# One-hot spread of the gates: a fixed order with score tiles between, strided PSUM columns, 52 instead of 43 score tiles ahead

## Chip, cores and metric

One core of one Trainium2 chip. The metric is the device time of one execution in microseconds: 2368.05 us, the median of three runs (2366.97 to 2370.98).

## What is computed

Two transformer blocks over 512 tokens of 1024 features, all in float32 accuracy (a matrix product is three products of high and low halves). The part that matters here is the first block's expert layer, which picks 16 of 16384 experts for each of 8 heads of each token:

```python
def peer_ffn(x, w_q, sub_keys, u, v):
    ...
        q = (xi @ w_q).reshape(n, PEER_HEADS, 2, PEER_KEY_DIM)
        s = jnp.einsum('nhpc,hpkc->nhpk', q, sub_keys).astype(jnp.float32)
        ts, ti = lax.top_k(s, PEER_TOPK)
        ...
        best_s, best_p = lax.top_k(cand_s, PEER_TOPK)
        idx = jnp.take_along_axis(cand_i, best_p, axis=-1)
        gate = jax.nn.softmax(best_s, axis=-1)
        act = jax.nn.gelu(jnp.einsum('nd,nhkd->nhk', xi, u[idx]).astype(jnp.float32), approximate=False)
        return jnp.einsum('nhk,nhkd->nd', (gate * act).astype(xi.dtype), v[idx])
```

An expert's number is 128 i1 + i2, two key numbers.

## The kernel before

The expert layer treats its tokens in two ways. For the first 384 tokens it computes **every** expert: 128 *U passes* (one score tile `pu`, 128 experts by 384 tokens, from the transposed `peer_u`; `upass`, 24 matmuls of 384 columns, then a Gelu on ScalarE) and 128 *V passes* (`vpass`, 18 matmuls of 512 columns into six PSUM accumulators `po`). Between them the scores are multiplied by G, a dense table of gates [i2, i1, token] that is zero nearly everywhere. The last 128 tokens are computed from gathered rows: 256 indirect DMAs (`gath`, tile `gr`, three buffers, issued by GpSimd), each followed by one VectorE operation.

In order of time: *routing* (query projections, scores, top-16; 24 U passes run beside it), the *spread* that builds G, the *V phase*. NG U passes run ahead of the V phase; their scores go to DRAM (`sd`) and come back (`gl`). In the V phase iterations below NG are V passes alone; from then on each iteration is a U pass and a V pass (*mixed*). VectorE's order is written out by hand there: for each iteration the low half `ulo` of a U weight tile, then some gathers' operations, then `ge`, `vlo`, `cl`, which feed the next V pass. The number of gathers per iteration is spread evenly by

```python
        total = (128 - NG) * 2 + NG * WV - GE
            cost += 2 if i >= NG else WV
            while done < min(256, 256 * cost // total):
```

with WV = 0.5 and GE = 4. Every weight tile is loaded raw by SyncE's queue, cast to its high half by ScalarE (`uhi`, `vhi`) and subtracted to its low half by VectorE or GpSimd (`eng`).

The spread (`spread`, L1093 to L1145) builds G from 768 small matmuls: for each token two products (high and low half of the gates) of a one-hot matrix of i2 (`oa`) with a scaled one-hot matrix of i1 (`ob`), 128 by 128 each, in float16. VectorE writes `bh`, `eql`, `bl` for 64 tokens at a time and `oa`, `ob` for 8 (two buffers). Four tokens share one PSUM bank `pq`, each in 128 neighbouring columns; ScalarE copies the bank into `gs` or `gk` with the token innermost, so that neighbouring PSUM columns land 64 elements apart. `gs` and every second block go to DRAM (`gd`). The scheduler of the framework sets the order here; `ahead(1)` offers it 12 U passes between, and `ahead(NG)` the rest.

Of the kernel before, what the change touches and what calls it, by code (L numbers as in the profile page):

```python
# [20 lines left out]
D = 1024  # L21
# [10 lines left out]
# the even tokens, and the odd ones  # L32
# [133 lines left out]
def _nabias(rpb):  # L166
    """[4 blocks, 8 heads, 128 queries (c, r), 256 keys (c, r)]: the bias, or NEG outside the window"""
# [14 lines left out]
def _sib():  # L182
    """pairs (j, i) whose blocks of s are siblings, s = 1..32"""
    j = np.arange(128)[:, None]
    i = np.arange(128)[None, :]
    return np.stack([(((j // s) ^ (i // s)) == 1).astype(np.float32) for s in (1, 2, 4, 8, 16, 32)], 1)


def program(tc, a, dbg=None):
# [54 lines left out]
    def rstd_of(pool, ps, n, feat, eps, tag="rs", bufs=1, b=None):  # L244
        """-2 feat / sqrt(ps / feat + eps), with one Newton step; the gains carry the factor -1 / (2 feat)"""
# [10 lines left out]
    def warm_rs(after):  # L256
        """the table of the norms, ahead of one"""
# [6 lines left out]
    # ---------------------------------------------------------------- first block, mixing  # L264
# [11 lines left out]
    NG = 43  # L276
    GT = 3
    GN = 3
    OAN = 8
    PQB = 6  # L280
    # the order of the first projection's parts; the last one runs after the others' pools are closed
# [20 lines left out]
    with ExitStack() as es:  # L302
# [10 lines left out]
        def ada_steps():  # L313
            """the conditioning columns: products of rows of the transposed weights with the vectors, and their sums"""
# [29 lines left out]
        def weights():  # L344
            """the next tile of weights; the ones after it are on their way"""
# [14 lines left out]
        # the norm's factor scales the products' columns; the operands hold the gains alone  # L360
# [26 lines left out]
        def rs_columns():  # L387
            """the factor of a token's row, for tiles that have the tokens on the partitions"""
# [14 lines left out]
        def rotate(raw, j):  # L403
            """rotary embedding of a projected tile"""
# [103 lines left out]
        for o in order[:NT]:  # L508
            if o == 'z':
                x0.close()  # L510
                zp = x0.enter_context(tc.tile_pool(name="z", bufs=1, reuse_waits="tile"))
                # lambda
# [8 lines left out]
                V.tensor_scalar(lam, lam, 0.8 - 0.6, -1.0, op0=OP.add, op1=OP.mult)   # -lambda  # L521
# [14 lines left out]
        # ------------------------------------------------ gated linear attention, both directions  # L536
# [12 lines left out]
        def gla_pair(hp):  # L549
# [9 lines left out]
            def diag(h):  # L559
                """the 128 x 128 blocks on the diagonal of A^T"""  # L560
# [79 lines left out]
            # the meta tokens: forward, from the end of their decay to the start of the sequence  # L640
# [42 lines left out]
    # ------------------------------------------------ conditioning of the second block  # L683
# [6 lines left out]
    scl = const.tile([128, 3, KT], F32, name="scl")   # norm gain * (1 + scale): latent 1, context, latent 2  # L690
# [48 lines left out]
        # ------------------------------------------------ differential attention  # L739
# [123 lines left out]
    def shifted(pool, src, n, sc_, sh, rs, hi, lo):  # L863
        """src * gain * rs + shift in two halves"""
# [21 lines left out]
    with ExitStack() as es:  # L886
# [5 lines left out]
        # the context: its norm now, its keys and values behind the output projection  # L892
# [54 lines left out]
    # ------------------------------------------------ experts: scores and routes  # L947
# [20 lines left out]
    # ------------------------------------------------ experts: every expert for the first 384 tokens  # L968
# [10 lines left out]
    def upass(i):  # L979
        wh, wl = us.pop(i)  # L980
        p = psU.tile([128, ND], F32, name="pu")
        for k in range(KT):
            w_ = (wh[:, k * 128:k * 128 + 128], wl[:, k * 128:k * 128 + 128])
            mm3(p, w_, (hn[0][:, k, :ND], hn[1][:, k, :ND]), k == 0, k == KT - 1)
        ge = up.tile([128, ND], F32, name="ge", bufs=4)
# [6 lines left out]
    with ExitStack() as es:  # L992
# [7 lines left out]
        def route(h):  # L1000
            """the 16 best pairs of a head, as two key numbers, for every token"""
            tf = wp.tile([128, 4, 2, 16], BF16, name="tf")
            V.tensor_copy(tf, ti[:, :, 2 * h:2 * h + 2])
            # a pair (a, b) of ranks can be among the best 16 only if (a + 1) (b + 1) <= 16
# [28 lines left out]
            for c in range(2):  # L1033
                # the best 8 have ranks below 8
# [35 lines left out]
        # gates: a softmax over the 16 of each head, the first of which is the largest  # L1070
# [6 lines left out]
    # the last 64 tokens' part stays on chip  # L1077
# [13 lines left out]
    def spread(nt):  # L1091
        """G[i2, i1, n], through DRAM: a sum of products of one-hot rows, the gates scaled and in two halves"""
# [4 lines left out]
        # i1 = 16 a + b; every number twice, so that the last step of an operand is one element  # L1097
        iu = rp.tile([128, 2, 128], U32, name="iu", bufs=1)
        V.tensor_copy(iu[:, 0], p[:, 0:128])
        V.tensor_scalar(iu[:, 1], iu[:, 0], 15, None, op0=OP.bitwise_and)  # L1100
        tw = [rp.tile([128, 128, 2], F16, name=f"tw{j}", bufs=1) for j in range(5)]
        d2 = [128, 128, 2]
        V.tensor_copy(tw[1], iu[:, 1, :, None].to_broadcast(d2))
        V.tensor_tensor(tw[0], p[:, 0:128, None].to_broadcast(d2), tw[1], op=OP.subtract)
        S.copy(tw[2], p[:, 128:256, None].to_broadcast(d2))
        S.mul(tw[3], p[:, 256:384, None].to_broadcast(d2), GS)
        V.scalar_tensor_tensor(tw[4], p[:, 256:384, None].to_broadcast(d2), GS, tw[3], op0=OP.mult, op1=OP.subtract)
        for n0 in range(0, 128, 64):
# [690 lines left out]
```

## Time and profile before

| | |
|---|---|
| median of three runs | 2368.05 us |
| span of the profiled execution (its own time; it shows no other) | 2382.4 us |
| mean granted TensorE clock over it | 0.978 |
| TensorE busy | 2258.9 us, 95% |
| VectorE, ScalarE, GpSimd busy | 72%, 42%, 30% |
| the spread, first to last one-hot product | 653.3 to 792.2 us |
| first V pass, last V pass | 805.9 us, about 1715 us |

Busy time of TensorE is no measure by itself, since matmuls overlap; the starts of consecutive matmuls show its pace. The clock column tells where the engine ran at half speed.

### The profile page before, as it was taken

How to read it: one execution, taken by the hardware profiler on the slowest of the kernel's cores; microseconds unless marked ns; L12 is line 12 of the kernel's file. 1: busy time of each engine (PE TensorE's matmuls, PEld its weight loads, DVE VectorE, ACT ScalarE, POOL GpSimd, SP SyncE). 2: the span in 40 equal slices, each digit the busy share in tenths (PEclk: the TensorE clock that was granted, in tenths of full speed). 3: DMA queues.
4: the chain of work that ended last, by engine and by line, in shares of the span. 5: the costliest groups of instructions: out<-in, count | busy, mean ns of one | idle time of the engine just before them, and what ended most of it. 6: DMA issues, size and time to landing. Idle time of an engine off the chain costs nothing.

```text
span 2382.4 us, 30940 instructions
## 1 busy us (share of the span) xinstructions
PE 2258.9 (95%) x11457; PEld 1895.9 (80%) x11457; DVE 1722.6 (72%) x3152; ACT 993.4 (42%) x1439; POOL 703.3 (30%) x428
## 2 busy tenths in 40 slices
PE   7999898999888999999999999999998999999997
PEld 6876466899767888899999987889877677788885
DVE  8997776799988677777777767778679565433334
ACT  5337774333277533333333323333443654322322
POOL 2132213344333311234343444443463023000001
PEclk9999998999989999999999999999999999999999
DMA  7760022533255899889999888889521221322320
GB/s 252 254 212 9 1 102 76 183 124 102 98 194 229 323 307 305 292 312 327 313 315 326 293 279 286 293 296 339 173 98 53 69 93 50 136 98 89 106 89 36
DMA packets 153831, 448.69 MB, mean 188 GB/s; under 512 B 14768, under 2 KB 58160, under 8 KB 151888
## 3 DMA queue, kind: packets, MB, share of 16 engines
q1 hardware_dynamic: 116768, 312.36, 37.5%
q0 software_dynamic: 36912, 134.37, 16.4%
q8 instruction: 89, 1.46, 0.2%
q14 instruction: 62, 0.51, 0.1%
HBM read 415.15 MB, written 31.52 MB: 187 GB/s over the span
## 4 chain that ended last, share of the span: by engine, by line
PE 73%; DVE 12%; DMA 6%; issue 4%; ACT 3%; POOL 2%; DVEq 0%; POOLq 0%; SPq 0%; ACTq 0%
PE pu L223 6%; PE pu L221 6%; PE po L221 6%; PE po L222 6%; PE po L223 6%; PE pu L222 6%; DMA gr<-in_v,idx 5%; PE psB L221 3%; PE psB L222 2%; PE psB L223 2%; PE pm L222 2%; PE pm L223 2%; PE pm L221 2%; PE pa L221 2%; PE pa L222 2%
## 5 line engine op out<-in xcount | busy, mean ns | idle before, releaser
L223 PE MATMUL pu<-hn,ulo 128*128 128x384 f32 x1024 | 353.4, 345 | 12.5 <-POOL ulo L234 12.5
L221 PE MATMUL pu<-hn,uhi 128*128 128x384 f32 x1024 | 354.2, 346 | 0.8 <-ACT uhi L233 0.8
L222 PE MATMUL pu<-hn,uhi 128*128 128x384 f32 x1024 | 351.7, 343 | 0.0
L221 PE MATMUL po<-vhi,ch 128*128 128x512 f32 x768 | 302.8, 394 | 9.4 <-ACT ch L1187 9.4
L222 PE MATMUL po<-vlo,ch 128*128 128x512 f32 x768 | 302.3, 394 | 0.4
L223 PE MATMUL po<-vhi,cl 128*128 128x512 f32 x768 | 300.8, 392 | 0.0
L234 POOL TENSOR_TENSOR wlo<-wraw,whi 128x1024 fp32r<-128x1024 f32 x57 | 144.5, 2540 | 398.0 <-ACT whi L233 328.2
L233 ACT CAST whi<-wraw 128x1024 fp32r<-128x1024 f32 x109 | 114.0, 1049 | 345.0 <-PE pm L222 126.7
L1206 POOL DMA_INDIRECT gr<-in_u,idx x128 | 148.2, 1158 | 344.8 <-DVE aact L1211 324.8
L1206 POOL DMA_INDIRECT gr<-in_v,idx x128 | 177.4, 1386 | 231.9 <-DVE acc L1220 190.7
L233 ACT CAST uhi<-uraw 128x1024 fp32r<-128x1024 f32 x129 | 135.6, 1051 | 248.9 <-PE pu L222 215.0
L1220 DVE SCALAR_TENSOR_TENSOR acc<-gr,aact,acc 128x1024 f32<-128x1024 f32 x126 | 159.0, 1280 | 87.7 <-DMA gr<-in_v,idx 87.1
L223 PEld LDWEIGHTS pu<-hn,ulo 128*128 128x128 f32 x1024 | 194.9, 190 | 13.4 <-POOL ulo L234 13.1
L221 PEld LDWEIGHTS pu<-hn,uhi 128*128 128x128 f32 x1024 | 194.9, 190 | 4.9 <-ACT uhi L233 0.9
L222 PEld LDWEIGHTS pu<-hn,uhi 128*128 128x128 f32 x1024 | 194.5, 190 | 4.1
L1176 ACT CAST vhi<-vraw 128x1024 fp32r<-128x1024 f32 x128 | 134.4, 1050 | 149.5 <-PE po L223 92.0
L1188 DVE TENSOR_TENSOR vlo<-vraw,vhi 128x1024 fp32r<-128x1024 f32 x128 | 156.1, 1220 | 42.9 <-ACT vhi L1176 42.9
L234 DVE TENSOR_TENSOR wlo<-wraw,whi 128x1024 fp32r<-128x1024 f32 x52 | 63.5, 1222 | 160.7 <-ACT whi L233 160.6
L221 PEld LDWEIGHTS po<-vhi,ch 128*128 128x128 f32 x768 | 144.5, 188 | 40.9 <-ACT ch L1187 13.3
L1211 DVE CUSTOM_DVE_ANT_0 gr<-gr,hnat 128x1024 f32<-128x1024 f32 x128 | 153.7, 1220 | 27.8 <-DMA gr<-in_u,idx 27.5
L223 PEld LDWEIGHTS po<-vhi,cl 128*128 128x128 f32 x768 | 144.4, 188 | 35.1 <-DVE cl L1189 4.0
L234 POOL TENSOR_TENSOR ulo<-uraw,uhi 128x1024 fp32r<-128x1024 f32 x39 | 123.2, 3163 | 157.8 <-ACT uhi L233 149.0
(567 smaller groups left out, 5106.1 us busy)
## 6 DMA issues: line engine op xcount, KB each, us to landing
uraw<-in_ut SPq DMA_DIRECT2D x129, 512.0 KB, 5.1
vraw<-in_v SPq DMA_DIRECT2D x128, 512.0 KB, 5.6
aw<-in_ada SPq DMA_DIRECT2D x48, 512.0 KB, 4.9
gt<-gd SPq DMA_DIRECT2D x42, 480.0 KB, 7.3
wraw<-in_m SPq DMA_DIRECT2D x32, 512.0 KB, 3.7
xraw<-in_m SPq DMA_DIRECT2D x32, 512.0 KB, 4.2
gd<-gs SPq DMA_DIRECT2D x6, 2048.0 KB, 9.8
sd<-ge SPq DMA_DIRECT2D x43, 192.0 KB, 2.1
```

The lines of the kernel that those rows point to most:

```text
L221: PE.matmul(out, lhs[0], rhs[0], start=first, stop=False)
L222: PE.matmul(out, lhs[0], rhs[1], start=False, stop=False)
L223: PE.matmul(out, lhs[1], rhs[0], start=False, stop=last)
L233: S.copy(hi, raw)
L234: eng.tensor_sub(lo, raw, hi.bitcast(F32))
L1176: S.copy(wh, raw)
L1188: V.tensor_sub(wl, raw, wh.bitcast(F32))
L1206: G.indirect_dma_start(r, None, src, bass.IndirectOffsetOnAxis(ap=idx[:, j:j + 1], axis=0))
L1211: V.tensor_tensor_reduce(out=r, in0=r, in1=hnat, scale=1.0, scalar=0.0, op0=OP.mult, op1=OP.add, accum_out=aact[:, j:j + 1])
L1220: V.scalar_tensor_tensor(A, r, aact[:, j:j + 1], A, op0=OP.mult, op1=OP.add)
```

## The change

The spread and the U passes from number 24 to 51 become one pipeline whose order on VectorE, ScalarE and TensorE is the order of the program text (`manual_schedule`). U passes 24 and 25 run first. Then come 48 steps of 8 tokens; each holds 16 one-hot products and half a U pass (12 matmuls), in two alternations, so that 24 U passes run beside the spread; two more follow. The one-hot operands are made two steps ahead (three buffers), the row tables for 32 tokens at a time, and the U weights' low halves of these passes on VectorE, no longer on GpSimd. A token's product writes every fourth column of its PSUM bank, so that ScalarE reads the bank in order and writes runs of four tokens. The numbers `idx` for the gathers are computed in the fourth step. NG is 52 instead of 43; the V phase's code is unchanged.

```diff
-    NG = 43
+    NR = 26
+    NG = 52
...
-            us[i] = wsplit(up, a['ut'][i], bufs=2, tag="u", eng=G if 3 <= i < NG - 1 else V)
+            us[i] = wsplit(up, a['ut'][i], bufs=2, tag="u", eng=G if 3 <= i <= NR else V)
+
+    def prep_u_hi(i):
+        raw = up.tile([128, 1024], F32, name="uraw", bufs=3)
+        nc.sync.dma_start(raw, a['ut'][i])
+        us[i] = [up.tile([128, 1024], F32R, name=t, bufs=2) for t in ("uhi", "ulo")] + [raw]
+        S.copy(us[i][0], raw)
+
+    def prep_u_lo(i):
+        hi, lo, raw = us[i]
+        V.tensor_sub(lo, raw, hi.bitcast(F32))
...
+    def umm(i, p, ks):
+        wh, wl = us[i][:2]
+        for k in ks:
             w_ = (wh[:, k * 128:k * 128 + 128], wl[:, k * 128:k * 128 + 128])
             mm3(p, w_, (hn[0][:, k, :ND], hn[1][:, k, :ND]), k == 0, k == KT - 1)
...
+    CH = 32
...
+    def spread_ops(s):
+
+        if s * 8 % CH == 0:
+            spread_rows(s * 8)
...
+        oa = rp.tile([128, 8, 128], F16, name="oa", bufs=3)
...
+        ob = rp.tile([128, 2, 8, 128], F16, name="ob", bufs=3)
...
-                            PE.matmul(p[:, q * 128:q * 128 + 128], oa[:, q0 + q], ob[:, j, q0 + q], start=j == 0, stop=j == 1)
-                    S.mul(gs[:, :, n1 + q0:n1 + q0 + 4].rearrange("p a n -> p n a"), p.rearrange("p (n a) -> p n a", n=4),
-                          1.0 / GS)
...
+        pv = p.rearrange("p (a n) -> p n a", n=4)
+        for q in range(4):
             for j in range(2):
...
+                PE.matmul(pv[:, q], oa[:, q0 + q], ob[:, j, q0 + q], start=j == 0, stop=j == 1)
+        S.mul(gs[:, :, n1 + q0:n1 + q0 + 4], p.rearrange("p (a n) -> p a n", n=4), 1.0 / GS)
...
-    for nt in range(3):
-        for b, _ in enumerate(spread(nt)):
-            if b % 8 in (1, 5):
-                ahead(1)
...
-    ahead(NG)
...
+    NS = 48
+    with tc.manual_schedule(engines={e.engine for e in (nc.vector, nc.scalar, nc.tensor)}):
+        i0 = ges["next"]
+        for i in range(i0, NR):
+            prep_u(i + 1)
+            upass(i)
+        spread_pre(0)
+        spread_ops(0)
+        spread_ops(1)
+        ti = NR
+        held = None
+        for s in range(NS):
+            if s % 2 == 0:
+                if held is not None:
+                    ugelu(*held)
+                prep_u_hi(ti + 1)
+                held = ti, psU.tile([128, ND], F32, name="pu")
+            if s + 2 < NS:
+                spread_ops(s + 2)
+            if s % 2 == 0:
+                prep_u_lo(ti + 1)
+            if s % 16 == 12 and s < 32:
+                spread_pre(s // 16 + 1)
+            for q0 in (0, 4):
+                spread_mm(s, q0)
+                k0 = (s % 2) * 4 + q0 // 2
+                umm(*held, range(k0, k0 + 2))
...
+        ugelu(*held)
+        for i in range(ti, NG):
+            prep_u(i + 1)
+            upass(i)
```

TensorE in the middle of the spread, before: `oa` and `ob` are the one-hot operands of 8 tokens, numbered by buffer, `pq` their PSUM bank, `pu` a U pass's score tile.

```order
L222 MATMUL pu_6303<-hn1_2828,uhi_6138 128x384
L223 MATMUL pu_6303<-hn0_2827,ulo_6139 128x384
L1139 LDWEIGHTS oa_5834
L1139 MATMUL pq_5839<-ob_5836,oa_5834 128x128
L1139 LDWEIGHTS oa_5834
L1139 MATMUL pq_5849<-ob_5836,oa_5834 128x128
L221 MATMUL pu_6303<-hn0_2827,uhi_6138 128x384
```

The same engine in the changed kernel, between two banks of one step:

```order
L1179 MATMUL pq_5804<-ob_5751,oa_5749 128x128
L221 MATMUL pu_5759<-hn0_2827,uhi_5688 128x384
L222 MATMUL pu_5759<-hn1_2828,uhi_5688 128x384
L223 MATMUL pu_5759<-hn0_2827,ulo_5689 128x384
L221 MATMUL pu_5759<-hn0_2827,uhi_5688 128x384
L222 MATMUL pu_5759<-hn1_2828,uhi_5688 128x384
L223 MATMUL pu_5759<-hn0_2827,ulo_5689 128x384
L1179 LDWEIGHTS oa_5749
L1179 MATMUL pq_5820<-ob_5751,oa_5749 128x128
```

Before, the first products of both banks of the next 8 tokens stand after a few matmuls of a U pass, and the rest after a few more; now eight products and six U matmuls take turns throughout.

VectorE at the start of the spread, before (`tw` are the tokens' numbers and gates in float16, `eql`, `bh`, `bl` the row tables):

```order
L1116 TENSOR_TENSOR eql<-iota_5646,tw_5658 128x1024
L1114 TENSOR_TENSOR bh<-iotah,tw_5657 128x1024
L1107 SCALAR_TENSOR_TENSOR tw_5661<-pq,tw_5660 128x256
L1120 TENSOR_TENSOR bl<-eql,tw_5660 128x1024
L1120 TENSOR_TENSOR bl<-eql,tw_5661 128x1024
L1125 TENSOR_TENSOR oa<-iota_5646,tw_5659 128x1024
L1131 TENSOR_TENSOR ob<-bh,bl 128x1024 x2
L1125 TENSOR_TENSOR oa<-iota_5646,tw_5659 128x1024
L1131 TENSOR_TENSOR ob<-bh,bl 128x1024 x2
```

and in the changed kernel, from the row tables to the first low half of a U tile:

```order
L1142 TENSOR_TENSOR bh<-iotah,tw_5725 128x512
L1143 TENSOR_TENSOR eql<-iota_5646,tw_5726 128x512
L1146 TENSOR_TENSOR bl<-eql,tw_5728 128x512
L1146 TENSOR_TENSOR bl<-eql,tw_5729 128x512
L1157 TENSOR_TENSOR oa<-iota_5646,tw_5727 128x1024
L1162 TENSOR_TENSOR ob<-bh,bl 128x1024 x2
L1157 TENSOR_TENSOR oa<-iota_5646,tw_5727 128x1024
L1162 TENSOR_TENSOR ob<-bh,bl 128x1024 x2
L1157 TENSOR_TENSOR oa<-iota_5646,tw_5727 128x1024
L1162 TENSOR_TENSOR ob<-bh,bl 128x1024 x2
L971 TENSOR_TENSOR ulo<-uraw,uhi 128x1024
```

The row tables are half as long and come twice as often, and VectorE now has one `ulo` for every two steps between the one-hot operands.

## Rows read from the trace of the kernel before

**Rows 1.** Busy time by stretch: us, then PE, PEld, DVE, ACT, POOL busy, clock, DMA share, GB/s.

```profile
653.30:792.20 138.90, 114.54 (x1067) 97.35 (x1068) 113.97 (x172) 105.34 (x123) 57.38 (x12) 0.89 0.57 220
983.00:1284.00 301.00, 301.00 (x1514) 274.34 (x1513) 236.11 (x376) 108.08 (x145) 118.26 (x98) 1.00 0.90 314
1284.00:1706.00 422.00, 412.14 (x2017) 365.74 (x2016) 316.41 (x371) 138.11 (x192) 176.36 (x127) 1.00 0.83 293
```

**Rows 2.** Groups in 653.3 to 792.2: xcount, busy us, mean ns, idle before, releaser.

```profile
L1139 PE MATMUL pq<-ob,oa 128*128 128x128 f16 x768 | 65.8, 234 | 15.0 <-DVE ob L1131 15.0
L234 POOL TENSOR_TENSOR ulo<-uraw,uhi 128x1024 fp32r<-128x1024 f32 x12 | 57.4, 4794 | 77.1 <-ACT uhi L233 77.1
L223 PE MATMUL pu<-hn,ulo 128*128 128x384 f32 x98 | 38.6, 394 | 12.5 <-POOL ulo L234 12.5
L221 PE MATMUL pu<-hn,uhi 128*128 128x384 f32 x98 | 38.3, 391 | 0.0
L222 PE MATMUL pu<-hn,uhi 128*128 128x384 f32 x97 | 37.0, 382 | 0.0
```

**Rows 3.** Chain of waits in the spread: start us, us, what.

```profile
677.53 5.78 POOL ulo L234
785.08 1.52 PE pq L1139 x14
```

**Rows 4.** Timeline of TensorE at full clock: start us, us (pipelined), engine, line.

```profile
624.74 0.34 PE L221 MATMUL pu<-hn,uhi 128*128 128x384 f32 x1
625.27 0.34 PE L221 MATMUL pu<-hn,uhi 128*128 128x384 f32 x1
...
774.43 0.95 PE L1139 MATMUL pq<-ob,oa 128*128 128x128 f16 x14
775.20 0.42 PE L222 MATMUL pu<-hn,uhi 128*128 128x384 f32 x1
```

**Rows 5.** Timeline of VectorE, one group of 8 tokens to the next.

```profile
774.20 0.68 DVE L1125 TENSOR_TENSOR oa<-iota,tw 128x1024 f16<-128x1024 f16 x1
776.00 0.68 DVE L1125 TENSOR_TENSOR oa<-iota,tw 128x1024 f16<-128x1024 f16 x1
```

**Rows 6.** Durations of `ulo` over the run: ns min/median/max, first and last start.

```profile
L234 DVE TENSOR_TENSOR ulo<-uraw,uhi x90: 1209/1217/1225, 415.9 to 1691.8; 128x1024 fp32r<-128x1024 f32 x90
L234 POOL TENSOR_TENSOR ulo<-uraw,uhi x39: 2337/2404/11767, 442.6 to 794.8; 128x1024 fp32r<-128x1024 f32 x39
```

**Rows 7.** Timeline of ScalarE at the spread's end.

```profile
790.10 3.80 ACT L1140 ACTIVATE gk<-pq 128x512 f32<-128x512 f32 x4
793.69 1.07 ACT L233 CAST uhi<-uraw 128x1024 fp32r<-128x1024 f32 x1
```

**Rows 8.** Timeline of VectorE and TensorE from the gates to the first product.

```profile
640.78 0.67 DVE L1076 TENSOR_TENSOR gate<-gate,gz 128x512 f32<-128x512 f32 x1
644.59 1.65 DVE L1154 CAST idx<-i 128x128 int32<-128x128 f32 x1
648.62 3.44 DVE L1120 TENSOR_TENSOR bl<-eql,tw 128x1024 f16<-128x1024 f16 x2
653.33 0.28 PE L1139 MATMUL pq<-ob,oa 128*128 128x128 f16 x2 [3.15 <-DVE ob L1131]
```

**Rows 9.** Last operand of the first V pass, on VectorE.

```profile
803.30 0.55 DVE L1189 TENSOR_TENSOR cl<-gl,ch 128x384 fp32r<-128x384 f32 x1
```

**Rows 10.** One VectorE operation per V-phase iteration (V alone: `gl`; mixed: `ge`).

```profile
L1185 DVE TENSOR_TENSOR ge<-ge,gt x85: 480/491/564, 983.2 to 1705.6; 128x320 f32<-128x320 f32 x85
L1185 DVE TENSOR_TENSOR gl<-gl,gt x43: 483/485/494, 801.6 to 973.4; 128x320 f32<-128x320 f32 x43
1284.20 0.49 DVE L1185 TENSOR_TENSOR ge<-ge,gt 128x320 f32<-128x320 f32 x1 [0.62 <-ACT ge L986]
1326.01 0.49 DVE L1185 TENSOR_TENSOR ge<-ge,gt 128x320 f32<-128x320 f32 x1 [0.36 <-DMA vraw<-in_v]
1616.04 0.48 DVE L1185 TENSOR_TENSOR ge<-ge,gt 128x320 f32<-128x320 f32 x1
```

More of the change, by code (lines that the diff above doesn't have):

```diff
@@ L274, in psB @@
         return ps.tile([128, 512], F32, name="psB", bufs=4)
-    NG = 43
+    NR = 26
+    NG = 52
     GT = 3
     GN = 3
-    OAN = 8
     PQB = 6
@@ L979, in upass, with ugelu @@
     def upass(i):
-        wh, wl = us.pop(i)
         p = psU.tile([128, ND], F32, name="pu")
-        for k in range(KT):
+        umm(i, p, range(KT))
+        ugelu(i, p)
+    def umm(i, p, ks):
+        wh, wl = us[i][:2]
+        for k in ks:
             w_ = (wh[:, k * 128:k * 128 + 128], wl[:, k * 128:k * 128 + 128])
             mm3(p, w_, (hn[0][:, k, :ND], hn[1][:, k, :ND]), k == 0, k == KT - 1)
+        if KT - 1 in ks:
+            us.pop(i)
+    def ugelu(i, p):
         ge = up.tile([128, ND], F32, name="ge", bufs=4)
@@ L1089, in pairs, with spread_pre @@
         return ap.rearrange("p n (a b) -> p n a b", b=2)
-    def spread(nt):
+    CH = 32
+    tws = {}
+    def spread_pre(nt):
         i1, i2, g = (t[:, nt].rearrange("p h k -> p (h k)") for t in (*ij, gate))
@@ L1098, in spread @@
         iu = rp.tile([128, 2, 128], U32, name="iu", bufs=1)
+        tw = [rp.tile([128, 128, 2], F16, name=f"tw{j}", bufs=2 if j == 2 else 1) for j in range(5)]
+        d2 = [128, 128, 2]
         V.tensor_copy(iu[:, 0], p[:, 0:128])
+        S.copy(tw[2], p[:, 128:256, None].to_broadcast(d2))
+        S.mul(tw[3], p[:, 256:384, None].to_broadcast(d2), GS)
         V.tensor_scalar(iu[:, 1], iu[:, 0], 15, None, op0=OP.bitwise_and)
-        tw = [rp.tile([128, 128, 2], F16, name=f"tw{j}", bufs=1) for j in range(5)]
@@ L1147, in program, with spread_rows @@
-    for nt in range(3):
-        for b, _ in enumerate(spread(nt)):
-            if b % 8 in (1, 5):
-                ahead(1)
-    i1, i2, g = (t[:, 3].rearrange("p h k -> p (h k)") for t in (*ij, gate))
-    V.tensor_copy(gnat, g)
-    V.scalar_tensor_tensor(i1, i1, 128.0, i2, op0=OP.mult, op1=OP.add)
-    V.tensor_copy(idx, i1)
-    ahead(NG)
+        tws[nt] = tw
+    chunk, onehot, gsb = {}, {}, {}
+    def spread_rows(t):
+        tw = tws[t // 128]
+        ns = slice(t % 128, t % 128 + CH)
+        b4 = [128, CH, 8, 2]
+        bh = rp.tile([128, CH, 8, 2], F16, name="bh", bufs=1)
+        eq = rp.tile([128, CH, 16], F16, name="eql", bufs=1)
+        bl = rp.tile([128, 2, CH, 16], F16, name="bl", bufs=1)
+        V.tensor_tensor(bh, iotah[:, None].to_broadcast(b4), tw[0][:, ns, None, :].to_broadcast(b4), op=OP.is_equal)
+        V.tensor_tensor(pairs(eq), pairs(iota16[:, None, 0:16]).to_broadcast(b4), tw[1][:, ns, None, :].to_broadcast(b4),
+                        op=OP.is_equal)
+        for j in range(2):
+            V.tensor_tensor(pairs(bl[:, j]), pairs(eq), tw[3 + j][:, ns, None, :].to_broadcast(b4), op=OP.mult)
+        chunk[0] = bh, bl
@@ new lines, in spread_ops @@
+    def spread_ops(s):
+        if s * 8 % CH == 0:
+            spread_rows(s * 8)
+        bh, bl = chunk[0]
+        m, n1 = s * 8 % 128, s * 8 % CH
+        tw = tws[s // 16]
+        oa = rp.tile([128, 8, 128], F16, name="oa", bufs=3)
+        V.tensor_tensor(pairs(oa), pairs(iota16[:, None]).to_broadcast([128, 8, 64, 2]),
+                        tw[2][:, m:m + 8, None, :].to_broadcast([128, 8, 64, 2]), op=OP.is_equal)
+        ob = rp.tile([128, 2, 8, 128], F16, name="ob", bufs=3)
+        b4 = [128, 8, 8, 8, 2]
+        for j in range(2):
+            V.tensor_tensor(ob[:, j].rearrange("p n (a b c) -> p n a b c", a=8, c=2),
+                            bh[:, n1:n1 + 8, :, None].to_broadcast(b4),
+                            bl[:, j, n1:n1 + 8].rearrange("p n (b c) -> p n b c", c=2)[:, :, None].to_broadcast(b4),
+                            op=OP.mult)
+        onehot[s] = oa, ob
@@ new lines, in spread_mm @@
+    def spread_mm(s, q0):
+        oa, ob = onehot[s]
+        tb, n1 = s // 8, s % 8 * 8
+        if n1 + q0 == 0:
+            gsb[0] = gk if tb % 2 else rp.tile([128, 128, 64], F32, name="gs")
+        gs = gsb[0]
+        p = psR.tile([128, 512], F32, name="pq", bufs=PQB)
+        pv = p.rearrange("p (a n) -> p n a", n=4)
+        for q in range(4):
+            for j in range(2):
+                PE.matmul(pv[:, q], oa[:, q0 + q], ob[:, j, q0 + q], start=j == 0, stop=j == 1)
+        S.mul(gs[:, :, n1 + q0:n1 + q0 + 4], p.rearrange("p (a n) -> p a n", n=4), 1.0 / GS)
+        if n1 + q0 == 60 and tb < 5:
+            for q in range(0, 128, 64):
+                nc.sync.dma_start(gd[tb, :, q:q + 64], gs[:, q:q + 64])
@@ new lines, in program @@
+    NS = 48
[25 more added lines that the diff above has]
+                umm(*held, range(k0, k0 + 2))
+            if s % 2:
+                ti += 1
+            if s == 3:
+                i1, i2, g = (t[:, 3].rearrange("p h k -> p (h k)") for t in (*ij, gate))
+                V.tensor_copy(gnat, g)
+                V.scalar_tensor_tensor(i1, i1, 128.0, i2, op0=OP.mult, op1=OP.add)
+                V.tensor_copy(idx, i1)
+        ugelu(*held)
+        for i in range(ti, NG):
+            prep_u(i + 1)
+            upass(i)
```

37 lines of the change are left out of this document (removed).

## Prediction

> **What bounds the kernel now.** I read first the busy time by stretch. TensorE is the engine that is busy nearly throughout, so the question of each stretch is whether it runs without gaps at full clock. In the spread it does not: of 138.9 us it is busy 114.5, at a mean clock of 0.89 [rows 1]. In the first mixed part of the V phase (983 to 1284) it has no gap, and in the second (1284 to 1706) it lacks 10 us of 422.
>
> Next, what the work of the spread would cost at full clock. In the timeline three steps from one U matmul to the next take 0.53 us, 0.176 each; 14 one-hot products take 0.77 us until the next matmul starts, 0.055 each [rows 4]. The groups show 768 products and 293 U matmuls in this stretch, some 12 U passes [rows 2]. That is 768 x 0.055 + 293 x 0.176 = 42.2 + 51.6 = 93.8 us of work in 138.9 us: 45 us are waiting and half clock.
>
> What it waits for stands in the same groups and in the chain. The products wait 15.0 us for `ob` of VectorE, the U matmuls 12.5 us for `ulo` of GpSimd [rows 2]. GpSimd's subtraction takes 4794 ns on average there and up to 11.8 us, where its median over the run is 2404 [rows 2, 6], and it stands in the chain with 5.78 us at a time [rows 3]. After such a gap 14 products take 1.52 us, 0.109 each, the pace of the lower clock level, 1.2 GHz [rows 3].
>
> The V phase is bound by TensorE in its first half: 36 mixed iterations lie between the operations at 983.2 and 1284.2, 8.36 us each; iterations of V alone take (973.4 - 801.6) / 42 = 4.09 us [rows 10]. From 1284.2 on the gathers come from `peer_v`, and 48 iterations take 421.4 us, 8.78 each: 20 us over the pace of 8.36. In the worst stretch, 32 iterations from 1326.0 to 1616.0, it is 9.06 [rows 10]. There VectorE stands with gathers' operations in its queue ahead of the next V pass's operands.
>
> **The change, part by part.** *Start.* The gates are ready at 641.4 [rows 8]. Three transposes, the number and row tables and the first operands follow. Before, this took until 653.3, with the cast of `idx` (1.65 us) in it and one `bl` of 2.8 us instead of 0.6; two `bl` of 64 tokens took 3.44 us [rows 8]. The cast is moved to step 3, the tables are half as long, and GpSimd has no work left that stretches them. Without these 1.6 + 2.2 us and half of four 0.6 us tables, 1.2 us, the first product comes at about 648 us. TensorE has finished passes 24 and 25 by then and idles some 6 us, as it waits today; its first microseconds run at the lower level, which I price at 2 us.
>
> *The 48 steps.* One step is 16 x 0.055 + 12 x 0.176 = 0.88 + 2.11 = 2.99 us on TensorE. VectorE needs 1.80 us for `oa` and `ob` from one group to the next [rows 5], a quarter of four half-long row tables (4 x 0.33 / 4 = 0.33, my estimate from 0.6 us for the long ones), half an `ulo` (1.22 / 2 [rows 6]) and a sixteenth of some 1.5 us of number tables: 2.83 us. ScalarE needs two evictions, 0.95 us each at the old pattern's pace, and half of a cast and a Gelu (1.07 and, my estimate for the smaller tile, 0.5): 2.7 us [rows 7]. So TensorE bounds the step by a small margin, and operands two steps ahead give VectorE 6 us of play for its table steps. What a faster eviction saves on ScalarE is hidden behind TensorE. 48 steps are 143.5 us; with 2 us at the lower clock the spread ends at 648 + 145.5 = 793.5, where it ends today (792.2). Passes 50 and 51 (8.4 us) then cover most of the 11.7 us that the first V operands needed after the last product, 803.9 - 792.2 [rows 9]. The V phase starts at about 805, against 805.9: 1 us gained. If VectorE bounds with waits in its own chain, at 3.2 us a step, 10 us are lost.
>
> *NG.* At that moment 52 U passes are done instead of 43. Nine iterations become V alone: 9 x (8.36 - 4.09) = 38.4 us gained.
>
> *The gathers.* They are spread over a total cost of 174 instead of 187.5, so a mixed iteration takes 512 / 174 = 2.94 instead of 2.73. Queued behind each gather's operation on VectorE are the next V pass's operands, and TensorE waits for them. In the `peer_u` half VectorE is busy 236 of 301 us [rows 1], 6.56 us an iteration; 0.2 operations more make 6.8 of 8.36, and I expect no loss. In the `peer_v` half 128 gathers fill 43.5 iterations instead of 47. The nearest rows bound them: at today's mean excess (0.42 us) they lose 18 us, 2 less than now; at the worst stretch's 9.06, 30 us; if there each gather rather than each iteration sets the time, 9.06 x 2.94 / 2.73 = 9.76, 61 us. Nearly every iteration has three gathers now, with three buffers, so I take a value above 9.06: 9.2, 36 us, 16 more than now.
>
> *Strided columns.* No row of this trace has a matmul that writes other than neighbouring columns. I bound a product between 0.055 us, today's price (a gain has no reason: the same 128 columns pass), and 0.109 us, the price of one column per cycle of the lower level [rows 4, 3], and take 0.055, since this is the row of the same instruction at the same clock.
>
> The Trainium skill speaks against this: PSUM — Partial Sum Buffer, section Specifications (TRN2), says that PSUM has lines of 8 bytes and that any non-contiguous access pattern slows matmuls significantly. It gives no figure, and no run here shows it.
>
> **Sum**, against the profiled span of 2382.4 us: -1 (start) - 38.4 (nine passes) + 16 (gathers) = -23.4, 2359.0. The profiled span is 14 us above the median of the runs, so I carry the difference over: 2368.05 - 23.4 = **2344.6 us**.
>
> **Rivals.** *The products at half pace.* Each of the 768 strided products takes 0.109 us; a step is 3.85 us and TensorE still bounds it, so 768 x 0.054 = 41.5 us come on top: 2386, slower than before. It decides from 0.055 + 23.4 / 768 = 0.085 us a product on. For it: only every second of two columns that now pass together would. Against it: nothing in the trace, either way; ScalarE's and VectorE's patterns do not show what TensorE's output does. By the page named above this is the way it would go, if "significantly" means a factor of two.
>
> *The gathers take the bound.* At 9.76 us for the whole `peer_v` half the loss is 61 - 20 = 41 us: -39.4 + 41 = 2370, no change. For it: VectorE already waits there. Against it: after 1616 the iterations run at 8.1 with the same gathers [rows 10], (1705.6 - 1616.0) / 11.
>
> *The gathers lose no more than now*: -39.4 - 2, 2327. For it: the `peer_u` half has none with the same three buffers.
>
> **Chances.** The forecast, 2334 to 2360 with its unknowns: 0.49. Half pace: 0.20. Gathers as the bound: 0.14. No more loss: 0.13. A fixed order that holds TensorE up in a way not priced here: 0.04. A measurement can tell about 0.2% (5 us) from no change. Faster: 0.49 + 0.13 and small parts of the others, 0.67; slower: half pace and parts of the gathers and the rest, 0.24; between: 0.09. The range leaves out half of the half-pace case and of the lowest case: 2326 to 2386.
>
> **What would show it.** Right: TensorE's clock near 1.00 and no gap from about 650 to 805; U passes end every 6 us; a product starts 0.055 us after the last; V phase from about 805 with `gl` operations 52 times; no `ulo` on GpSimd after the first steps. Wrong: 14 or 8 products at 0.1 us each with the clock at 1.00; VectorE without idle time in the spread and TensorE waiting for `ob`; mixed iterations of 9 us or more, or such iterations already in the `peer_u` half.

## The result: 2.6% slower, and the profile after

The changed kernel takes 2429.74 us in the median (2420.25 to 2445.74), against 2369.52 us: a ratio of 1.0258, 95% interval 1.0203 to 1.0313. Forecast was 2344.6. Medians here and below are over all executions; ratios leave out those that were disturbed and compare with the kernel before as it ran beside them. The profiled execution spans 2423.2 us, 40.8 more than the one of before. It splits at three operations of VectorE, the first `gl`, the first `ge` and the last `ge` (before: [rows 10]).

| us | before | after | difference | forecast |
|---|---|---|---|---|
| to the first `gl` | 801.6 | 845.6 | +44.0 | -1 |
| V alone, 43 or 52 iterations | 181.6 | 217.0 | +35.4 | +36.8 |
| mixed, 84 or 75 | 722.4 | 684.4 | -38.0 | -59.2 |
| the rest | 676.8 | 676.2 | -0.6 | 0 |
| span | 2382.4 | 2423.2 | +40.8 | -23.4 |

(In the last column, +36.8 is nine iterations at 4.09; -59.2 is nine mixed ones at 8.36, less 16 for gathers.) Two places failed: the time up to the V phase, by 45 us, and the mixed iterations, by 21.

The changed kernel's busy time by stretch, for the spread and the V phase's two mixed parts (us, then PE, PEld, DVE, ACT, POOL busy, clock, DMA share, GB/s):

```profile
649.30:838.60 189.30, 189.07 (x1343) 173.60 (x1344) 138.70 (x223) 88.47 (x145) 3.02 (x3) 0.99 0.56 212
1062.00:1320.00 258.00, 257.32 (x1282) 232.04 (x1281) 203.80 (x327) 87.94 (x122) 106.28 (x87) 1.00 0.90 318
1320.00:1747.00 427.00, 398.58 (x1870) 343.99 (x1869) 305.74 (x357) 126.25 (x179) 192.83 (x129) 0.98 0.81 283
```

The spread is what was asked for: the clock is 0.99 instead of 0.89, and TensorE is busy 189.07 of 189.30 us, where it lacked 24 us [rows 1]. It still takes 189.3 us instead of 138.9. Its groups, and its chain of waits, say with what:

```profile
L1179 PE MATMUL pq<-ob,oa 128*128 128x128 f16 x767 | 101.9, 313 | 4.7 <-DVE ob L1162 4.7
L971 DVE TENSOR_TENSOR ulo<-uraw,uhi 128x1024 fp32r<-128x1024 f32 x24 | 29.4, 1225 | 17.1 <-ACT uhi L967 17.1
```

```profile
655.82 0.89 PE pq L1179 x8
656.70 0.18 PE pu L221
...
657.77 0.89 PE pq L1179 x8
```

The waits of [rows 2] are gone (of 15.0 us for `ob` are left 4.7, ahead of the first product, and no U matmul waits for GpSimd). Instead the chain is TensorE itself, from one eight of products to the next in 1.95 us. Its timeline at full clock:

```profile
743.85 1.05 PE L1179 MATMUL pq<-ob,oa 128*128 128x128 f16 x8
744.65 0.42 PE L221 MATMUL pu<-hn,uhi 128*128 128x384 f32 x1
744.92 0.34 PE L222 MATMUL pu<-hn,uhi 128*128 128x384 f32 x1
...
745.80 1.05 PE L1179 MATMUL pq<-ob,oa 128*128 128x128 f16 x8
```

Eight products take 0.80 us until the next matmul starts, 0.100 each, where [rows 4] have 0.055. The six U matmuls take 1.15 us, where 6 x 0.176 = 1.06 were forecast: the first after the products holds TensorE 0.27 us.

The starts of `gl` and `ge`, one per iteration, and the waits from 1320 to 1747 us (the `peer_v` half; total us, times, longest):

```profile
L1253 DVE TENSOR_TENSOR gl<-gl,gt x52: 481/487/494, 845.6 to 1052.8; 128x320 f32<-128x320 f32 x52
```

```profile
L1253 DVE TENSOR_TENSOR ge<-ge,gt x76: 477/485/493, 1062.6 to 1747.0; 128x320 f32<-128x320 f32 x76
1330.08 0.48 DVE L1253 TENSOR_TENSOR ge<-ge,gt 128x320 f32<-128x320 f32 x1
1742.91 0.48 DVE L1253 TENSOR_TENSOR ge<-ge,gt 128x320 f32<-128x320 f32 x1
```

```profile
DVE acc L1288 <- DMA gr<-in_v,idx: 115.4, 45, 6.6
PE po L221 <- ACT ch L1255: 26.7, 16, 3.1
```

A mixed iteration takes 684.4 / 75 = 9.13 us. The 31 with `peer_u` gathers take (1330.08 - 1062.6) / 31 = 8.63, 8 us in all over the pace of 8.36; the 43 with `peer_v` gathers 9.60, 53 us over it. (The one iteration after the last of them is shorter, 4.14.) VectorE waits for gathered rows, and TensorE for `ch`, which ScalarE casts from VectorE's `ge`.

### The profile page after: what moved, and what is told of

Same layout as the page of the kernel before. It is cut to its first block, busy times and chain, and to the rows that moved or that the text cites. A ratio compares the mean times of both kernels' runs of the same rounds, so it can differ in the third digit from the quotient of the medians.

```text
span 2423.2 us, 31002 instructions
## 1 busy us (share of the span) xinstructions
PE 2301.4 (95%) x11457; PEld 1925.6 (79%) x11457; DVE 1728.9 (71%) x3191; ACT 953.5 (39%) x1439; POOL 652.0 (27%) x413
## 4 chain that ended last, share of the span: by engine, by line
PE 52%; issue 11%; DMA 11%; DVE 7%; POOL 6%; ACT 1%; DVEq 0%; POOLq 0%; SPq 0%; ACTq 0%
DMA gr<-in_v,idx 10%; POOL gr L1274 5%; PE pq L1179 4%; PE po L223 3%; PE po L222 3%; PE po L221 3%; PE pu L221 3%; PE pu L223 3%; PE pu L222 3%; PE pm L222 2%; PE pm L223 2%; PE pm L221 2%; PE pa L222 2%; PE pa L221 2%; PE pa L223 2%
## 5 line engine op out<-in xcount | busy, mean ns | idle before, releaser
L223 PE MATMUL pu<-hn,ulo 128*128 128x384 f32 x1024 | 347.2, 339 | 0.0
L222 PE MATMUL po<-vlo,ch 128*128 128x512 f32 x768 | 307.2, 400 | 0.8
L223 PE MATMUL po<-vhi,cl 128*128 128x512 f32 x768 | 305.8, 398 | 0.1
L1274 POOL DMA_INDIRECT gr<-in_v,idx x128 | 192.3, 1502 | 224.5 <-DVE acc L1288 192.2
L1255 ACT CAST ch<-ge 128x384 fp32r<-128x384 f32 x76 | 39.0, 514 | 378.4 <-DVE ge L1254 378.4
L222 PEld LDWEIGHTS po<-vlo,ch 128*128 128x128 f32 x768 | 146.4, 191 | 37.9 <-DVE vlo L1256 9.5
```

The costliest lines, as they stand in the source:

```text
L222: PE.matmul(out, lhs[0], rhs[1], start=False, stop=False)
L223: PE.matmul(out, lhs[1], rhs[0], start=False, stop=last)
L1255: S.copy(ch, ge)
L1274: G.indirect_dma_start(r, None, src, bass.IndirectOffsetOnAxis(ap=idx[:, j:j + 1], axis=0))
```

## Experiments

| run | kernel | median us | ratio to before, 95% interval | mixed us | late issues |
|---|---|---|---|---|---|
| | the change | 2429.74 | 1.0258 (1.0203 to 1.0313) | 9.13 | 11 |
| 1 | neighbouring columns | 2397.75 | 1.0082 (1.0033 to 1.0131) | 9.33 | 11 |
| 2 | pairs of columns | 2397.02 | 1.0110 (1.0044 to 1.0177) | 9.16 | 10 |
| 3 | before, NG 52 | 2433.15 | 1.0259 (1.0169 to 1.0349) | 9.21 | 12 |
| 4 | four buffers, one accumulator | 2367.45 | 0.9960 (0.9923 to 0.9997) | 8.35 | 0 |
| 5 | one accumulator | 2391.24 | 1.0094 (1.0060 to 1.0128) | 8.63 | 0 |
| 6 | 2 and 4 together | 2329.18 | 0.9816 (0.9772 to 0.9860) | 8.35 | 0 |
| 7 | before, four buffers | 2367.49 | 0.9960 (0.9920 to 1.0001) | 8.35 | 0 |
| 8 | before, spaced columns | 2391.11 | 1.0022 (0.9968 to 1.0077) | 8.52 | 6 |
| 9 | `vlo` in another form | 2414.03 | 1.0145 (1.0047 to 1.0243) | 8.97 | 9 |
| 10 | four buffers, two accumulators | 2372.63 | 0.9973 (0.9933 to 1.0013) | 8.35 | 0 |
| 11 | 1 and 4 together | 2333.09 | 0.9818 (0.9748 to 0.9888) | 8.35 | 0 |
| 12 | a memset behind each accumulation | 2396.89 | 1.0129 (1.0095 to 1.0162) | 8.67 | 0 |

"Mixed" is the time from the first `ge` to the last, divided by the iterations between them; "late issues" are the `peer_v` gathers that GpSimd took over 3.5 us to issue. Both are read from the one profiled execution of each run; before, they are 8.60 us and 7. Runs not called "before" are edits of the change. The kernel before, run beside them, had medians of 2372.37 us (runs 1 to 4), 2380.49 (5 to 8), 2374.17 (9 to 11) and 2369.59 (12).

### The columns: runs 1, 2 and 8

Run 1 writes neighbouring columns, with the old eviction:

```diff
-        pv = p.rearrange("p (a n) -> p n a", n=4)
...
-                PE.matmul(pv[:, q], oa[:, q0 + q], ob[:, j, q0 + q], start=j == 0, stop=j == 1)
-        S.mul(gs[:, :, n1 + q0:n1 + q0 + 4], p.rearrange("p (a n) -> p a n", n=4), 1.0 / GS)
+                PE.matmul(p[:, q * 128:q * 128 + 128], oa[:, q0 + q], ob[:, j, q0 + q], start=j == 0, stop=j == 1)
+        S.mul(gs[:, :, n1 + q0:n1 + q0 + 4].rearrange("p a n -> p n a"), p.rearrange("p (n a) -> p n a", n=4), 1.0 / GS)
```

> The changed kernel with each token's product in 128 neighbouring columns again, and ScalarE's eviction writing 4-byte pieces as before; order and NG stay. Theory A (the spaced columns alone make a product cost 0.100 us instead of 0.055): eight products take 0.44 us until the next matmul starts instead of 0.80, a step 3.2 us instead of 3.905, the spread (649 to 838.6) ends some 35 us earlier, V phase from about 810 instead of 845.6, whole time about 35 us under that of the change. Rival B (the fixed alternation itself, with a change between float16 products and U matmuls every eight, sets the pace): products, steps and time stay as in the change, 0.80 us per eight.

Run 2 keeps the tokens together in the bank, but by two columns at a time:

```diff
-        pv = p.rearrange("p (a n) -> p n a", n=4)
+        pv = p.rearrange("p (b n c) -> p n b c", n=4, c=2)
...
-        S.mul(gs[:, :, n1 + q0:n1 + q0 + 4], p.rearrange("p (a n) -> p a n", n=4), 1.0 / GS)
+        S.mul(gs[:, :, n1 + q0:n1 + q0 + 4].rearrange("p (b c) n -> p b c n", c=2), p.rearrange("p (b n c) -> p b c n", n=4, c=2), 1.0 / GS)
```

> The changed kernel with each product written in pairs of neighbouring columns, every fourth pair (two columns, six skipped), ScalarE still writes runs of four tokens. Theory A1 (two columns that stand side by side go to PSUM together; spaced ones go one by one): 0.44 us per eight products as with neighbouring columns, V phase from about 810, eviction about 0.6 us, whole time some 35 us under the change. Theory A2 (any columns that are not all neighbours halve the pace): 0.80 us per eight, time as in the change.

TensorE in run 1, then in run 2, and run 2's evictions:

```profile
742.63 0.62 PE L1178 MATMUL pq<-ob,oa 128*128 128x128 f16 x8
743.05 0.42 PE L221 MATMUL pu<-hn,uhi 128*128 128x384 f32 x1
```

```profile
742.57 0.62 PE L1179 MATMUL pq<-ob,oa 128*128 128x128 f16 x8
743.00 0.42 PE L221 MATMUL pu<-hn,uhi 128*128 128x384 f32 x1
743.26 0.34 PE L222 MATMUL pu<-hn,uhi 128*128 128x384 f32 x1
```

```profile
L1180 ACT ACTIVATE gs<-pq x48: 597/600/604, 649.8 to 776.3; 128x512 f32<-128x512 f32 x48
```

Theory A, and of the two A1: 0.43 us per eight, with pairs as with neighbours; the runs are 32 and 33 us under the change. That is the price of spaced columns: 768 x (0.100 - 0.055) = 35 us. A pair of float32 columns is enough to escape it. The change of kind stays in both: the first U matmul holds TensorE 0.26 us instead of 0.176, 96 times, 8 us. The trace of before has this too, from the last of [rows 4] at 775.20 to the next matmul:

```profile
775.46 0.33 PE L223 MATMUL pu<-hn,ulo 128*128 128x384 f32 x1
```

Run 8 puts the spaced columns and the new eviction into the kernel before:

```diff
-                            PE.matmul(p[:, q * 128:q * 128 + 128], oa[:, q0 + q], ob[:, j, q0 + q], start=j == 0, stop=j == 1)
+                            PE.matmul(p.rearrange("p (a n) -> p n a", n=4)[:, q], oa[:, q0 + q], ob[:, j, q0 + q], start=j == 0, stop=j == 1)
...
-                    S.mul(gs[:, :, n1 + q0:n1 + q0 + 4].rearrange("p a n -> p n a"), p.rearrange("p (n a) -> p n a", n=4),
+                    S.mul(gs[:, :, n1 + q0:n1 + q0 + 4], p.rearrange("p (a n) -> p a n", n=4),
```

> The kernel before with every fourth column and the eviction in runs of four tokens, old order, NG 43. Theory A (each product 0.100 instead of 0.055 us) has 768 x 0.045 = 35 us more work in a spread of 138.9 us that had 45 us of waits and half clock: between 0 us (all of it in the waits) and 35 us slower. Rival H (the shorter eviction, 0.6 instead of 1.11 us, frees buffers and makes up for it): faster than before.

Its spread, and 14 spaced products in it:

```profile
654.60:800.30 145.70, 140.41 (x1067) 125.15 (x1067) 120.40 (x172) 74.21 (x123) 32.80 (x12) 0.99 0.54 210
```

```profile
770.74 1.70 PE L1139 MATMUL pq<-ob,oa 128*128 128x128 f16 x14
772.20 0.42 PE L221 MATMUL pu<-hn,uhi 128*128 128x384 f32 x1
```

It takes 145.7 us instead of 138.9, with the clock at 0.99 instead of 0.89: 28 of the 35 us fall into what had been waits and half clock. Neither faster nor slower can be told. The same price is hidden in the old order and exposed in one without waits. The 14 spaced products take 1.46 us. So six more than eight cost 0.66 us, 0.11 each, and with neighbouring columns (0.77 - 0.43) / 6 = 0.057: within a row of products the spaced ones run at about half pace, and the 0.100 is an average that holds the cheaper first and last.

### NG and the gathers' buffers: runs 3, 4, 5, 7 and 10

Run 3 is the kernel before with `NG = 52`.

> The kernel before with NG = 52 alone. Nine more U passes ahead of the V phase cost about 38 us there and save 9 x (8.36 - 4.09) = 38 us in it, if the mixed iterations keep their length. Theory C (with 2.94 gathers per mixed iteration and three buffers the gathers set the pace): mixed iterations average 9.1 us as in the change instead of 8.6, so about 36 us slower than before, some 2404. Rival D (the longer mixed iterations of the change come from something else): 8.6 us, time within 5 us of before.

```profile
L1185 DVE TENSOR_TENSOR ge<-ge,gt x76: 478/485/559, 1067.3 to 1757.9; 128x320 f32<-128x320 f32 x76
```

Theory C: 690.6 / 75 = 9.21 us. With neither fixed order nor spaced columns the time is that of the change, 29 us over the expected 2404: the first `ge` comes 84 us later than in [rows 10], where 75 were reckoned (38 for the passes, 37 for V alone), 8 us lie in the mixed iterations (9.21 for 9.1), and the other 12 between executions. That the times agree is chance: nine passes ahead of the V phase in the old order stand here for the dear products there. Run 2 has the same NG, three buffers and the fixed order, and its first `ge` comes 42 us earlier:

```profile
L1253 DVE TENSOR_TENSOR ge<-ge,gt x76: 480/485/494, 1025.0 to 1711.8; 128x320 f32<-128x320 f32 x76
```

It is 36 us faster in the median. So in these runs passes ahead gain where they fill TensorE's waits in the spread (run 2), and not where they come on top (run 3). Run 4 gives the gathers a fourth buffer:

```diff
-    acc = [vp.tile([128, D], F32, name=f"acc{j}") for j in range(2)]
+    acc = [vp.tile([128, D], F32, name="acc0")]
...
-        r = vp.tile([128, D], F32, name="gr", bufs=3)
+        r = vp.tile([128, D], F32, name="gr", bufs=4)
...
```

(The last dots stand for the lines that accumulate into the one tile and leave out the sum of the two.)

> The changed kernel with four buffers for gathered rows instead of three; one accumulator instead of two makes the room. Theory C1 (a gather's way from a free buffer to its landing, times three buffers, sets one gather per 3.3 us in the peer_v half): with four buffers one per 2.8 us, mixed iterations near 8.4 to 8.6 us instead of 9.1, 40 to 55 us less time than the change. Rival C2 (the DMA queues are full and bound the gathers): mixed iterations within 0.1 us of the change's, time within 10 us.

```profile
L1253 DVE TENSOR_TENSOR ge<-ge,gt x76: 484/492/493, 1063.1 to 1689.3; 128x320 f32<-128x320 f32 x76
```

626.2 / 75 = 8.35 us, the pace of TensorE; 62 us are gone, with the same gathers over the same DMA queues. C2 falls. Two things were changed, so run 5 has one accumulator and three buffers, and run 10 two accumulators and four buffers (`vraw` with two instead of three).

> The changed kernel with one accumulator instead of two for the gathered rows and still three buffers: the control for the run with four buffers, which changed both. Theory C1 (the fourth buffer made the gain there): mixed iterations 9.1 to 9.4 us, time within 15 us of the change. Rival E (the single accumulator made it): 8.35 us, some 60 us less.

> The changed kernel with four buffers for gathered rows and still two accumulators; the room comes from the V weights' raw tiles, two buffers instead of three, which may cost something in the iterations of V alone. Theory C1 (a fourth buffer lets VectorE find its rows landed even when an issue is late): mixed iterations 8.35 to 8.45 us. Rival N (two accumulators bring the long issues back, and they cost as before): mixed iterations 8.7 us or more.

Run 5's starts of `ge` and issues, then run 10's:

```profile
L1253 DVE TENSOR_TENSOR ge<-ge,gt x76: 479/485/493, 1059.3 to 1706.9; 128x320 f32<-128x320 f32 x76
1327.32 0.49 DVE L1253 TENSOR_TENSOR ge<-ge,gt 128x320 f32<-128x320 f32 x1 [0.24 <-ACT ge L1005]
1702.49 0.49 DVE L1253 TENSOR_TENSOR ge<-ge,gt 128x320 f32<-128x320 f32 x1
```

```profile
L1274 POOL DMA_INDIRECT gr<-in_v,idx x128: 932/946/1971, 1320.3 to 1695.9; - x128
```

```profile
L1253 DVE TENSOR_TENSOR ge<-ge,gt x76: 491/493/494, 1065.2 to 1691.4; 128x320 f32<-128x320 f32 x76
L1274 POOL DMA_INDIRECT gr<-in_v,idx x128: 933/938/1742, 1314.4 to 1674.0; - x128
```

Run 10 shows that the fourth buffer does it without the single accumulator. Run 5 came out between its two theories: 38 us less than the change, which neither foretold. Its `peer_u` half is as slow as in the change (8.65 us), but its `peer_v` half takes (1702.49 - 1327.32) / 43 = 8.72 instead of 9.60, and its longest issue 1.97 us instead of 5.02. That led to the late issues, below. Of the 62 us some 38 so go with the late issues, and the other 24 or so are waits that three buffers leave even without them (8.63 against 8.35 us); no issue is late with four buffers, so whether four would hide a late one is not shown.

Run 7 is run 4's edit on the kernel before.

> The kernel before with four buffers for gathered rows and one accumulator. Theory C1: its mixed iterations go from 8.60 to 8.36 us, 20 us less, about 2348 to 2350 for the median; the change with pairs and four buffers then stays faster by 15 to 30 us, which is what the fixed order and nine passes are worth. Rival G (before, the waits for gathers were hidden): within 5 us of before.

```profile
L1185 DVE TENSOR_TENSOR ge<-ge,gt x85: 491/491/566, 990.1 to 1691.6; 128x320 f32<-128x320 f32 x85
```

Mixed iterations fall to 701.5 / 84 = 8.35 us as foretold, 21 us less than in [rows 10], but the median is 2367.49, not 2348 to 2350, and the ratio does not tell it from before. The first `ge` is 7 us later than in the profile of before, whose span was already 14 us over its median; how much of its 20 us of excess the median execution has, no run shows. The ten executions of run 7 lie within 9 us, those of before that its ratio rests on between 2364.95 and 2399.69: the loss to gathers may differ from one to the next.

### The late issues: runs 9 and 12

Before and after, the `peer_v` gathers' issues on GpSimd (ns min/median/max; 7 are late before, 11 after):

```profile
L1206 POOL DMA_INDIRECT gr<-in_v,idx x128: 932/944/5016, 1282.3 to 1689.8; - x128
```

```profile
L1274 POOL DMA_INDIRECT gr<-in_v,idx x128: 935/958/5016, 1320.8 to 1736.4; - x128
```

In the change 11 of them take 4.17 or 5.02 us. One, with VectorE's timeline beside it:

```profile
1438.59 1.74 POOL L1274 DMA_INDIRECT gr<-in_v,idx  x1 [3.53 <-DVE acc L1288]
1440.63 4.17 POOL L1274 DMA_INDIRECT gr<-in_v,idx  x1 [0.30 <-issue]
1445.11 0.94 POOL L1274 DMA_INDIRECT gr<-in_v,idx  x1 [0.30 <-issue]
```

```profile
1439.43 1.27 DVE L1288 SCALAR_TENSOR_TENSOR acc<-gr,aact,acc 128x1024 f32<-128x1024 f32 x1
1440.63 0.48 DVE L1253 TENSOR_TENSOR ge<-ge,gt 128x320 f32<-128x320 f32 x1
...
1443.91 1.27 DVE L1288 SCALAR_TENSOR_TENSOR acc<-gr,aact,acc 128x1024 f32<-128x1024 f32 x1
```

Ordinary issues end some 0.9 us after the end of the VectorE operation in which they start: the one at 1438.59 ends at 1440.33, 0.90 us after the next accumulation began (1439.43). The late one starts with `ge` and ends 0.89 us after the start of the next `acc`: it was held off over five operations (`ge` twice, `vlo`, `cl`, `ulo`). Ten of the 11 start within 0.01 us of `ge`; the other, like four of the seven before, starts 0.35 us into the accumulation ahead of `ge`, waits for it and then loses in the same way, 5.02 us in all. The Trainium skill (SBUF — State Buffer, section Who interferes with whom) has a rule for the ordinary wait: a VectorE instruction with two inputs in SBUF and a GpSimd instruction that reads SBUF exclude each other, and the later one waits to the end of the other. The trace agrees for the ordinary issues (a gather takes its numbers from the tile `idx`); that a wait goes on over several instructions, this section of the Trainium skill does not say. Run 9 changes the form of one of the five:

```diff
-        V.tensor_sub(wl, raw, wh.bitcast(F32))
+        V.scalar_tensor_tensor(wl, raw, 1.0, wh.bitcast(F32), op0=OP.mult, op1=OP.subtract)
```

> The changed kernel (three buffers, two accumulators) with one operation in the V phase in another form: the V weights' low half vlo is a scalar_tensor_tensor (raw times 1 minus the high half), the form that the accumulation has, instead of a tensor_tensor; the values are the same. In the change 11 gathers of the peer_v half are issued by GpSimd in 4.2 us instead of 0.94; each long one starts as VectorE's run of tensor_tensor operations ge, ge, vlo, cl, ulo starts, and ends 0.9 us into the accumulation behind it. Theory L (a tensor_tensor run on VectorE holds GpSimd's issue off, and a scalar_tensor_tensor does not): no gather in the peer_v half takes over 3 us, and 20 to 35 us are gained on the change, as with the single accumulator. Rival M (the long issues come from the DMA queues or from the accumulators): 8 to 12 long ones again, time within 10 us of the change.

```profile
L1274 POOL DMA_INDIRECT gr<-in_v,idx x128: 932/946/5013, 1319.9 to 1720.0; - x128
```

Nine late issues of 4.16 to 5.01 us remain: theory L falls. The form of this operation is not what matters (both forms have two inputs in SBUF); two late issues fewer are worth some 6 of the 16 us under the change (2 x 3.2), whose four executions lie 25 us apart. Run 12 shifts the starts instead:

```diff
+    gpad = vp.tile([128, 16], F32, name="gpad")
...
             V.scalar_tensor_tensor(A, r, aact[:, j:j + 1], A, op0=OP.mult, op1=OP.add)
+        V.memset(gpad, 0.0)
```

> The changed kernel (three buffers, two accumulators, tensor_tensor for vlo) with a tiny memset on VectorE behind each of the 128 accumulations of the peer_v half: it moves ge and the operations behind it against GpSimd's issues by some 0.1 us per accumulation and nothing else. In the change, 10 of 11 long issues (4.17 us instead of 0.94) start within 0.01 us of ge; issues that start 0.04 us ahead or 0.35 us behind take 0.94. Theory L2 (the coincidence of the two starts makes them long): at most three long issues, and 20 to 38 us gained, as with one accumulator. Rival M2 (two alternating accumulators make them long, whenever they start): 8 to 12 long ones again, time within 10 us of the change.

```profile
L1275 POOL DMA_INDIRECT gr<-in_v,idx x128: 932/954/1830, 1318.2 to 1695.8; - x128
```

```profile
L1290 DVE MEMSET gpad<- x128: 72/72/72, 1324.9 to 1703.4; 128x16 f32 x128
```

As theory L2 has it: 128 operations of 0.07 us more on VectorE, no late issue, 33 us less time. (The profiled execution is the fastest of the four, as in run 5; that the others have no late issue is not shown.) Run 5 fits: on one accumulator, accumulations in a row start 1.31 us apart instead of 1.20, which moves the issues against `ge`, and none starts within 0.01 us of it. But the rule is not complete. In the traces of all these kernels 51 of the 55 `peer_v` issues that start within 0.01 us of `ge` are late; the other four take 0.94 us, and there it is `ge` that is held up, as in run 8:

```profile
1543.25 0.53 DVE L1185 TENSOR_TENSOR ge<-ge,gt 128x320 f32<-128x320 f32 x1
1543.25 0.94 POOL L1206 DMA_INDIRECT gr<-in_v,idx  x1 [0.30 <-issue]
```

And in the change 12 issues that wait for the accumulation ahead of `ge` go on as soon as it ends, where the one of 5.02 us did not. Why a request that loses to `ge` also loses at the four boundaries behind it stays open.

### Both causes removed: runs 6 and 11

> The changed kernel with products in pairs of columns and four buffers for gathered rows. If the two causes are separate (A1 and C1): V phase from about 808, mixed iterations 8.35 us, whole time 2367 - 36 = about 2331. Rival F (with the spread shorter something else becomes late in the V phase): mixed iterations longer than 8.5 us or the time over 2345.

> The changed kernel with neighbouring columns (ScalarE writes 4-byte pieces again), four buffers and one accumulator. Against the run with pairs and four buffers (2329) it tells what the eviction in runs of four tokens is worth. Theory O (ScalarE's evictions are hidden behind TensorE in the fixed order): within 5 us of 2329. Rival P (the longer eviction holds up the banks): spread over 160 us and 8 us or more slower.

Run 6's `pq` and `ge`, then run 11's evictions:

```profile
L1179 PE MATMUL pq<-ob,oa x768: 218/219/330, 651.5 to 804.6; 128*128 128x128 f16 x192
```

```profile
L1253 DVE TENSOR_TENSOR ge<-ge,gt x76: 485/491/493, 1029.4 to 1655.6; 128x320 f32<-128x320 f32 x76
```

```profile
L1179 ACT ACTIVATE gs<-pq x48: 1086/1102/1177, 648.7 to 775.2; 128x512 f32<-128x512 f32 x48
```

The causes are separate: 2329.18 against an expected 2331, the fastest kernel here. It is 38.3 us under run 7, which has the same four buffers in the old order: what the fixed order, NG and the lighter eviction are worth together. The longer eviction (1.10 instead of 0.60 us) in run 11 goes with 4 us more, within theory O and hardly clear of the scatter: it is hidden behind TensorE, and the reason for spacing the columns was worth next to nothing.

## Why the prediction was wrong

- **The step that failed first is the price of a strided product.** "Take 0.055, since this is the row of the same instruction at the same clock": it is not the same instruction where its output pattern differs. It measured 0.100, and within a row of products 0.11, which was the upper bound. The rival that held it was right in sign, place and nearly in size: 35 us for 41.5 forecast. Its chance of 0.20 was set too low, since the trace spoke for neither end. The Trainium skill (PSUM — Partial Sum Buffer, section Specifications (TRN2)) has the rule for it: any non-contiguous access pattern slows matmuls significantly. The trace agrees for every fourth column (0.100 against 0.055 us) and not for pairs, which are non-contiguous too and cost nothing (run 2).
- **The step of 2.99 us lacked a term.** A U matmul behind products of the other kind takes 0.26 us: 8 us in 96 changes. The trace of before shows it, and it is missing from the 93.8 us reckoned there as well. 35 + 8 are 43 of the 45 us lost before the V phase.
- **The gathers were sized too low.** 9.2 us was taken for the `peer_v` half, and no loss for the other; measured 9.60 and 8.63, together 61 us over TensorE's pace where 36 were forecast (the short last iteration gives 4 back). The mechanism behind the 53 us of the `peer_v` half was half missed. Three buffers were named, but not that GpSimd's issues come late: 11 x (4.17 - 0.94) = 36 us. Run 5, without them, is (9.60 - 8.72) x 43 = 38 us shorter there. The row with its 5016 ns maximum was there before, and was not read. The rival "gathers as the bound" had 9.76.
- **The two rivals were priced as if one excluded the other.** -39.4 + 41.5 + 41 = +43 us by the text's own terms; the spans differ by +40.8. That these come so close is partly luck: the rivals measured 35 and 37 us (the mixed iterations, -38.0, against -75.2 without losses), 6 and 4 less than priced, and the 8 us for the change of kind make up for it. The range ended at one of them alone.
- **Right:** the start (first product at 649.3, 648 forecast), V alone (+35.4 for +36.8), a spread without waits at full clock, no `ulo` on GpSimd in it, evictions hidden. Without gather losses and with products at 0.055 the sum is -39.4; run 6 less run 7 is -38.3. Here too misses cancel in part: by spans the two differ by +5.6 us up to the first `gl` (-1 forecast), +33.7 in V alone (+36.8), -75.3 in the mixed iterations (-75.2) and -2.4 behind them (0). Run 7's starts of `gl`, then run 6's:

```profile
L1185 DVE TENSOR_TENSOR gl<-gl,gt x43: 481/485/493, 806.9 to 980.3; 128x320 f32<-128x320 f32 x43
L1253 DVE TENSOR_TENSOR gl<-gl,gt x52: 481/485/494, 812.5 to 1019.6; 128x320 f32<-128x320 f32 x52
```

- Of the 85 us between 2344.6 and 2429.74 the spans hold 64. The forecast started from the median of 2368.05 on the ground that the profiled execution of before stands 14 us over it; that of the change stands 6.5 us under its own median, and this makes the other 21. Why single executions stand so differently stays open.

## What to carry to other kernels

An operation whose access pattern changes has no row yet: take both bounds seriously, and when the price falls on the engine that has just been freed of waits, count it in full. Where work is packed closer (more gathers per iteration), look at how long each stage of their chain takes at worst (max beside median of issues), and add one buffer before judging the rest. Terms on different stretches add; price them together.

## What was not expected of the hardware

- A float16 product into every fourth float32 column takes 0.100 us in eights (0.11 within a row), into pairs or neighbours 0.055, at clock 1.00.
- GpSimd's issue of a gather takes 0.94 us, and 4.17 in 51 of 55 cases when it starts within 0.01 us of the first of five VectorE operations; a start 0.07 us later (at 1623.66 in the change) is ordinary, 1.22 us. A 0.07 us memset that moves the starts is worth 33 us in this kernel.
- Four instead of three buffers of gathered rows bring a mixed iteration from 9.13 to 8.35 us, at a DMA share that had been 0.81.
